# A hybrid S5, attention and mixture-of-experts layer: the scan dealt out in single instructions, biases later and on another queue, copies on another engine

## The chip, the cores and the metric

The kernel runs on one core of a Trainium2 chip. The metric is the device time of one execution in microseconds (us). The kernel before has a median of 1299.4 us over three runs (1301.35, 1297.85 and 1299.4).

The engines are named as the profile names them: PE is TensorE (PEld its weight loads), DVE is VectorE, ACT is ScalarE, POOL is GpSimd, SP is SyncE. In this kernel SP issues nearly all transfers and computes nothing; POOL issues a few.

## The reference, cut to what matters

There are 256 latent tokens and 256 context tokens of 1024 channels, one layer, batch 1, all in float32.

```python
h  = modulate(rmsnorm(x, norm1_g), sh1, sc1)        # sh, sc, g: from silu(c) @ w_mod + b_mod
hc = modulate(rmsnorm(ctx, norm1_g), sh1c, sc1c)
proj = h @ w_in            # columns: S5 input 512 | K 128 | V 128 | Q 512 | gates 2048
y = s5_mixer(proj[:, :512], ...)    # diagonal complex scan, 32 groups x 64 states, both directions
o = attention(q, k_all, v_all)      # 8 heads of 64, 2 KV heads, 512 keys, softmax
s = gelu(y); s = s * sigmoid(s @ w_glu + b_glu)
merged = sigmoid(gate_a) * (s @ w_ssm_out) + sigmoid(gate_b) * (o @ w_attn_out)
x = x + g1 * (merged @ w_out)
h2 = modulate(rmsnorm(x, norm2_g), sh2, sc2)
f = top-4-of-32 experts: gu = h2 @ w_gate_up[e] + b_gate_up[e]
                         act = (clip(up) + 1) * clip(gate) * sigmoid(1.702 gate)
                         act @ w_down[e] + b_down[e], weighted
out = rmsnorm(x + g2 * f, final_norm_g)
```

The experts' weights are 32 times 12 MB and are the bulk of the traffic.

## The kernel before

**Stages.** A first part (to about 135 us) loads x, ctx and the small parameters, builds the tables of the S5 part, and projects the S5 input, K, V and Q. A long middle part, the loop `for u in range(16)`, interleaves the gate projection with attention and with the S5 part. Then come a tail of attention chunks, eight *branches* (four output pieces of `w_ssm_out`, four of `w_attn_out`, each 24 matmuls), the output projection, the router, and the 32 experts.

**Memory.** There are 24 pages of 1 MB (128 x 2048 float32). A fixed list of transfers, the stream, holds every large weight tile in order of use: 8 gate tiles of `w_in`, `w_glu`, the tiles of `w_ssm_out`, `w_attn_out` and `w_out`, then the experts. When a page is given back (`release`, `used`), the next item of the stream is loaded into it by a DMA on SP. SP works through its DMAs in program order (`load`, L104), so a DMA that waits for a page holds up those behind it.

**Order.** From the middle part on, PE, DVE and ACT keep the order in which the program is written (`Pinned`, L49; `tmatmul`, L97; `ttrans`, L100). The rows of the profile therefore carry these helpers' lines, and what an instruction is must be told from its operands and its shape.

**Exactness.** A product is made of three fp32r products of halves: ACT copies a weight tile into a rounded `hi`, DVE subtracts it to get `lo`, and `mm3` issues hi*hi, hi*lo, lo*hi. A gate tile has two halves of 128 output columns, called units 0 to 15. A unit is 24 matmuls and needs two hi copies on ACT and two lo subtractions on DVE, each 128x512 (`gate_split`), a unit ahead of its use (`next_split`). `wsplit` does the same for the eight pieces n = 0 to 7 of the branches, with one copy and one subtraction of 128x1024. Its two buffers alternate, so the copy of piece n waits until PE has finished branch n - 2.

**The loop.** A unit u does, in this order: the normalization of the last attention chunk (`attn_norm`: reciprocal and multiply on DVE, then PE transposes), the split for unit u+1, `gate_mm` of its own unit, a modulation tile, and further pieces. From u = 3 on it does one attention chunk c = u - 3: score matmuls, row maximum on DVE (`smx`, the reduce), exp on ACT. The S5 scan stands in it as follows. At u = 2, `scan_up` issues 20 DVE instructions in a row (five levels of `cmul_add`, of 1024 columns falling to 64). From u = 3 to 9 the *pieces* follow, four DVE instructions at a time, two or three times a unit. At u = 10 the rest and `scan_out` follow: two copies of 64x992 on DVE and two on ACT, which lay out the states for the readout. At u = 11 `shift_logits` takes a small transposed copy, `shT`, to PE.

**Biases.** `bias_steps` is a generator. For n = 0, 1 (`b_gate_up`) and 2 (`b_down`) it issues three loads of 128 KB on POOL into one buffer, then makes, for each of two column halves, a bf16 copy on ACT, a subtraction on DVE, a copy, a subtraction and a copy. Each depends on the one before. The loop takes one step of it at each of three places per unit from u = 3 on, and what is left after it. The sums are needed only by the experts. POOL's queue also holds the 24 transfers of `Rd`, by which a kernel of the S5 part is spread over the partitions.

Of the kernel before, what the change touches and what calls it, by code (L numbers as in the profile page):

```python
# [12 lines left out]
F32R = mybir.dt.float32r  # L13
# [16 lines left out]
P_QT, P_M, P_A, P_SU, P_S, P_RO, P_RT, P_GL, P_BP = 2, 10, 3, 3, 10, 12, 14, 15, 3  # L30
# [3 lines left out]
def hybrid_block(ctx: ExitStack, tc: tile.TileContext, a: dict, out: bass.AP):  # L34
# [720 lines left out]
    S.activation(hH.bitcast(F32R), hT[1], AF.Copy)  # L755
    V.tensor_sub(hL.bitcast(F32R), hT[1], hH)
# [4 lines left out]
    mod_load(2)  # L761
    kv_proj(1, 1)
    mod_tile(False)
    w_tables(4)
    renew(13, "r")
    renew(10, "r")

    wgh, wgl_ = [pg(p_).rearrange("p (j k f) -> p j k f", j=2, k=8) for p_ in (13, 10)]

    def gate_split(i, j, parts=(0, 1)):  # L770
        for part in parts:
            for k in range(0, 8, GK):
                sl = slice(k, k + GK)
                src, hi, lo = loaded["gate", i][:, sl, 128 * j:128 * j + 128], wgh[:, j, sl], wgl_[:, j, sl]
                if part:
                    V.tensor_sub(lo.bitcast(F32R), src, hi)
                else:
                    S.activation(hi.bitcast(F32R), src, AF.Copy)

    gate_split(0, 0)  # L780
    gate_split(0, 1)
    used("gate", 0)
# [93 lines left out]
    def cmul_add(h_out, h_in, v_in, lv, n, t1, t2):  # L876
        lr_ = LS[:, lv, 0].unsqueeze(1).to_broadcast([128, n, 2, 32])
        li_ = LS[:, lv, 1].unsqueeze(1).to_broadcast([128, n, 2, 32])
        V.tensor_mul(t1, h_in, lr_)
        V.tensor_mul(t2, h_in[:, :, ::-1], li_)  # L880
        V.tensor_add(t1, t1, v_in)
        V.tensor_add(h_out, t1, t2)
# [15 lines left out]
    vb = vv[1].rearrange("p (b i) r g -> p i b r g", i=4)  # L900
    Sb, Hb, tb1, tb2 = [pg(8, 512 * i, 512).rearrange("p (s r g) -> p s r g", s=8, r=2) for i in range(4)]

    def scan_pieces():
        for i in range(1, 4):
            yield lambda i=i: cmul_add(Sb, Sb if i > 1 else vb[:, 0], vb[:, i], 0, 8, tb1, tb2)
        for b in range(8):
            if b:
# [3 lines left out]
        for i in range(3):  # L911
            yield lambda i=i: cmul_add(vb[:, i], vb[:, i - 1] if i else Hb, vb[:, i], 0, 8, tb1, tb2)
# [876 lines left out]
```

## Time and profile before

| | before |
|---|---|
| median of 3 runs | 1299.4 us |
| the profiled execution | 1298.59 us |
| its span, first to last instruction | 1296.9 us |
| mean granted clock of TensorE | 0.977 |
| busy PE / DVE / ACT | 90% / 32% / 14% |
| DMA moved | 462.55 MB, mean 357 GB/s |

All times of the trace count from the start of the span. The views used below are the page's chain of waits (the work that ended last, followed back from the end), the same chain in a stretch of time, a table of stretches (busy time of each engine, granted clock, DMA), the timeline of one engine (start, busy time, what it is, count, and in brackets the idle time before it and what ended that), the groups of instructions by line and shape, and the DMA issues. Instructions of one engine overlap a little, so that a row's duration can be some 0.1 us longer than the distance to the next row.

### The profile page before, as it was taken

Reading aid. Unit: us, or ns where it says so; the run is one execution under the profiler, and the core shown is the slowest. Engines: PE = TensorE matmul, PEld = TensorE weight load, DVE = VectorE, ACT = ScalarE, POOL = GpSimd, SP = SyncE. Lnnn points to the kernel's source line nnn. Section 1 sums busy time; section 2 is a strip of 40 time slices with the busy share of each in tenths; the row PEclk is TensorE's granted clock in tenths of the full one; section 3 lists DMA queues with packets and bytes.
Section 4 is the critical chain, followed back from the end, with each engine's and each line's share of the span. In section 5 each row is a group of like instructions: output and inputs, shape, how many; then the busy total and the mean of one; then the engine's idle time right before and its main releaser. Section 6 shows DMA issues by size and latency. Waiting matters only on the chain.

```text
span 1296.9 us, 16241 instructions
## 1 busy us (share of the span) xinstructions
PE 1172.1 (90%) x6791; PEld 540.0 (42%) x6792; DVE 414.5 (32%) x893; ACT 181.9 (14%) x350; POOL 50.0 (4%) x80
## 2 busy tenths in 40 slices
PE   3999685889989999999999998989898989899886
PEld 2775474769633333333333232323232323233224
DVE  4998886565322111211111211112111111111211
ACT  3142243552110000000000000000000000000001
POOL 1201032002000000000000000000000000000000
PEclk9999887989989999999999999999999999999998
DMA  9957267478799999999999999999999999999995
GB/s 279 311 192 251 99 144 145 151 284 338 273 376 418 417 417 418 417 417 417 417 416 417 417 417 417 418 417 417 417 418 417 418 416 417 416 417 416 416 386 194
DMA packets 119135, 462.55 MB, mean 357 GB/s; under 512 B 20669, under 2 KB 42345, under 8 KB 84242
## 3 DMA queue, kind: packets, MB, share of 16 engines
q1 hardware_dynamic: 117138, 457.13, 89.6%
q0 software_dynamic: 1872, 4.33, 1.6%
q8 instruction: 55, 0.90, 0.3%
q14 instruction: 22, 0.18, 0.0%
q10 hardware_dynamic: 48, 0.01, 0.0%
HBM read 459.89 MB, written 1.54 MB: 356 GB/s over the span
## 4 chain that ended last, share of the span: by engine, by line
DMA 45%; PE 43%; DVE 7%; ACT 2%; issue 2%; POOL 0%; SPq 0%; DVEq 0%; POOLq 0%; ACTq 0%
PE bk L97 41%; DMA pg<-in_w_gate_up_dram 28%; DMA pg<-in_w_down_dram 16%; DVE pg L49 5%; PE bk L100 3%; ACT pg L49 2%; DMA pg<-in_b_gate_up_dram 1%; DMA pg<-in_w_mod_dram 1%; DVE smx L49 1%; ACT L49 0%; DVE rsn_t L49 0%; DVE rs_t L49 0%; DVE gate L49 0%; DVE ssum L49 0%; DVE gs__2716 L49 0%
## 5 line engine op out<-in xcount | busy, mean ns | idle before, releaser
L97 PE MATMUL bk<-pg,pg 128*64 128x512 f32 (+7 forms) x5456 | 1004.7, 470 | 70.9 <-DMA pg<-in_w_down_dram 29.5
L97 PEld LDWEIGHTS bk<-pg,pg 128*64 128x64 f32 (+3 forms) x5456 | 452.1, 152 | 565.0 <-issue 360.9
L49 ACT ACTIVATE pg<-bk 128x512 f32<-128x512 f32 (+4 forms) x154 | 76.3, 522 | 746.2 <-PE bk L100 677.9
L49 DVE TENSOR_SCALAR pg<-bk 128x512 f32<-128x512 f32 x64 | 44.2, 691 | 295.3 <-PE bk L97 295.3
L49 DVE TENSOR_TENSOR pg<-pg,pg 128x1024 f32<-128x1024 f32 (+9 forms) x144 | 122.8, 881 | 36.5 <-ACT pg L49 33.3
L49 ACT ACTIVATE pg<-pg 128x512 f32<-128x512 f32 (+9 forms) x118 | 76.5, 670 | 263.3 <-DVE pg L49 231.5
L49 DVE TENSOR_TENSOR pg<-bk,shT 128x512 f32<-128x512 f32 x32 | 22.1, 691 | 268.1 <-PE bk L97 268.1
L49 DVE TENSOR_TENSOR pg<-bk,pg 128x512 f32<-128x512 f32 (+4 forms) x52 | 32.1, 619 | 227.7 <-PE bk L97 224.5
L100 PE MATMUL bk<-ident,pg 128*128 128x128 f32 x448 | 72.8, 291 | 21.4 <-DVE pg L49 14.0
L100 PEld LDWEIGHTS bk<-ident,pg 128*128 128x128 f32 x448 | 50.8, 145 | 82.7 <-issue 43.0
L97 PE MATMUL bk<-pg 64*128 64x512 f32 (+1 forms) x368 | 70.3, 484 | 0.0
L97 PEld LDWEIGHTS bk<-pg 64*128 64x128 f32 (+1 forms) x368 | 19.9, 159 | 50.0 <-issue 50.0
L49 DVE TENSOR_TENSOR pg<-pg 128x512 f32<-128x512 f32 (+3 forms) x89 | 37.3, 434 | 3.8 <-ACT pg L49 3.0
L1643 POOL DMA_DIRECT2D pg<-g2d x2 | 1.3, 642 | 883.8 <-PE bk L97 883.8
L97 PE MATMUL bk<-pg,selB 128*64 128x512 bf16 (+1 forms) x196 | 34.4, 388 | 0.0
L49 DVE SCALAR_TENSOR_TENSOR pg<-pg 128x512 f32<-128x512 f32 (+3 forms) x67 | 30.3, 458 | 6.6 <-DMA pg<-in_x_dram 4.8
L97 PE MATMUL bk<-pg,scond 128*32 128x256 f32 (+1 forms) x256 | 27.4, 525 | 2.5 <-DMA pg<-in_w_mod_dram 2.5
L49 DVE TENSOR_SCALAR pg<-iot,posp,gate 128x128 f32<-128x128 f32 x64 | 18.9, 339 | 0.0
L49 ACT ACTIVATE pg<-bk,smx 128x512 f32<-128x512 f32 x16 | 11.0, 688 | 35.9 <-DVE smx L49 35.8
L49 DVE TENSOR_SCALAR pg<-iot,posp,rs 128x64 f32<-128x64 f32 x64 | 15.7, 307 | 0.1
L97 PEld LDWEIGHTS <-selB 128*64 128x64 bf16 x196 | 9.0, 109 | 16.1 <-issue 15.9
L49 DVE COPY pg<-bk 128x512 f32<-128x512 f32 (+1 forms) x24 | 14.5, 610 | 3.4 <-PE bk L100 2.9
(151 smaller groups left out, 192.0 us busy)
## 6 DMA issues: line engine op xcount, KB each, us to landing
pg<-in_w_gate_up_dram SPq DMA_DIRECT2D x256, 1024.0 KB, 19.9
pg<-in_w_down_dram SPq DMA_DIRECT2D x127, 1024.0 KB, 20.1
pg<-in_w_mod_dram SPq DMA_DIRECT2D x16, 1024.0 KB, 5.9
pg<-in_w_in_dram SPq DMA_DIRECT2D x13, 1024.0 KB, 10.1
pg<-in_w_mod_dram SPq DMA_DIRECT2D x16, 512.0 KB, 9.4
pg<-in_w_out_dram SPq DMA_DIRECT2D x4, 1024.0 KB, 8.2
pg<-Rd POOLq DMA_DIRECT2D x16, 128.0 KB, 11.0
pg<-in_w_ssm_out_dram SPq DMA_DIRECT2D x2, 1024.0 KB, 5.1
```

The costliest lines, as they stand in the source:

```text
L49: i = f(*ar, **kw)
L97: pinned(T.matmul(*ar, **kw))
L100: pinned(T.transpose(*ar))
L1643: G.dma_start(late["g2"][:, 512 * j:512 * j + 512], g2d[j:j + 1].to_broadcast([128, 512]))
```

## The change

- **Scan.** `scan_up` and the pieces become one generator that yields after every DVE instruction. `scan_some(22)` takes instructions until their columns (in units of 64, plus 2 for each) come to 22: once at u = 2, twice a unit from u = 3 on, the rest at u = 10.
- **Whole gate tiles.** `N_WHOLE = 2`: units 0 to 3 multiply the loaded tile with `hT[1]` in plain float32, eight matmuls a unit, without a split. The split ahead of `q_proj(0)` goes; the split of h (`hH`, `hL`, 128x2048) moves from ahead of `kv_proj(0, 1)` to u = 1 (ACT) and u = 2 (DVE). Pages 13 and 10 carry modulation tiles in the meantime, and modulation tiles stand at other units. The biases of the modulation (`mod_bias`) move to u = 4.
- **Split order.** The hi copies of unit u+1 now stand ahead of `attn_norm` on ACT.
- **Copies.** The multiply of `attn_norm` moves from DVE to ACT; the two large copies of `scan_out` move from DVE to ACT, and two small ones from ACT to DVE.
- **Biases.** The loads go by SP. The steps begin at u = 9 (two a unit), go on with four after each branch's `wsplit`, and the rest stands after the branches. The zeroing on POOL is done once.

Cut to its core, with the loop's rows for modulation and the old page renewals left out:

```diff
-P_QT, P_M, P_A, P_SU, P_S, P_RO, P_RT, P_GL, P_BP = 2, 10, 3, 3, 10, 12, 14, 15, 3
+P_QT, P_M, P_A, P_S, P_RO, P_RT, P_GL, P_BP, P_B, P_SC, N_WHOLE = 2, 10, 3, 10, 12, 14, 15, 3, 9, 22, 2
...
-    S.activation(hH.bitcast(F32R), hT[1], AF.Copy)
-    V.tensor_sub(hL.bitcast(F32R), hT[1], hH)
     kv_proj(0, 1)
...
-    gate_split(0, 0)
-    gate_split(0, 1)
-    used("gate", 0)
     q_proj(0)
...
             for p in (0, 2, 3):
-                load_g(raw[32 * p:32 * p + 32], src)
-            for _ in range(4):
+                load(raw[32 * p:32 * p + 32], src)
+            for _ in range(3):
                 yield
...
     def cmul_add(h_out, h_in, v_in, lv, n, t1, t2):
-        V.tensor_mul(t1, h_in, lr_)
+        yield V.tensor_mul(t1, h_in, lr_), n
...
+    def scan_some(cols):
+        while cols > 0:
+            step = next(scan_left, None)
+            if step is None:
+                return
+            cols -= step[1] + 2
...
     def scan_out():
         for r in range(2):
-            V.tensor_copy(Hn[0:64, :, r, 1:32].rearrange("p g c -> p c g"), vv[1][0:64, 0:31, r])
+            S.activation(Hn[0:64, :, r, 1:32].rearrange("p g c -> p c g"), vv[1][0:64, 0:31, r], AF.Copy)
...
-            S.activation(Hn[64:128, :, r, 31:32].rearrange("p g c -> p c g"), h0[64:128, :, r], AF.Copy)
+            V.tensor_copy(Hn[64:128, :, r, 31:32].rearrange("p g c -> p c g"), h0[64:128, :, r])
...
         for k in range(8):
-            mm3(gbk[0][:, 256 * j:256 * j + 256], wgh[:, j, k], wgl_[:, j, k], hH[:, k], hL[:, k], k == 0, k == 7)
+            o = gbk[0][:, 256 * j:256 * j + 256]
+            if i < N_WHOLE:
+                mm(o, loaded["gate", i][:, k, 128 * j:128 * j + 128], hT[1][:, k], k == 0, k == 7)
+            else:
+                mm3(o, wg[0][:, j, k], wg[1][:, j, k], hH[:, k], hL[:, k], k == 0, k == 7)
...
-        V.tensor_scalar(pb, pb, ssum[:, c_i:c_i + 1], None, op0=ALU.mult)
+        S.activation(pb, pb, AF.Copy, scale=ssum[:, c_i:c_i + 1])
...
     for u in range(16):
+        next_split(u + 1, 0)
         attn_norm(n_attn - 1)
-        if u:
-            next_split(u + 1, 0)
-        if P_SU <= u < P_S:
-            n_scan = scan_some(1)
-        if u:
-            next_split(u + 1, 1)
+        next_split(u + 1, 1)
+        if u > 2:
+            scan_some(P_SC)
         gate_mm(u // 2, u % 2)
-        if u > 2:
-            next(bias_left, None)
...
         if u == P_QT:
             for i in range(2):
                 q_T(i)
                 k_T(i)
-            scan_up()
-        if P_SU <= u < P_S:
-            n_scan = scan_some(1)
+            V.tensor_sub(hL.bitcast(F32R), hT[1], hH)
+        if u > 1:
+            scan_some(P_SC)
...
-        if u > 2:
+        if u >= P_B:
             next(bias_left, None)
...
-    for _ in bias_left:
-        pass
...
         wsplit()
+        for _ in range(4):
+            next(bias_left, None)
...
+    for _ in bias_left:
+        pass
     release(0, 1, 10, 13)
```

Three places show how this moves instructions. The first is DVE between the transposes of q and k (u = 2) and the splits that follow. Before, these are the end of the scan's first part and its first piece (pg_68 and pg_62 are its pages, LS its multipliers), and behind them the lo subtractions of unit 3 (pg_1004):

```order
L49 TENSOR_TENSOR LS<-pg_62 128x64 [waits DVE_49]
L49 TENSOR_TENSOR pg_68<-pg_69,LS 128x512 x2
L49 TENSOR_TENSOR pg_68<-pg_68,pg_69 128x512 [waits DVE_49]
L49 TENSOR_TENSOR pg_68<-pg_68 128x512 [waits DVE_49]
L49 TENSOR_TENSOR pg_1004<-pg_83,pg_1003 128x512 [waits DMAHW5_49,DMAHW2_49,Activation_49]
L49 TENSOR_TENSOR pg_1004<-pg_83,pg_1003 128x512 [waits Activation_49]
```

After, with pg_309 as `hL` and pg_1243 as the lo buffer:

```order
L49 TENSOR_TENSOR pg_309<-pg_63,pg_308 128x2048
L49 TENSOR_TENSOR pg_62<-pg_68,LS 128x1024 x2
L49 TENSOR_TENSOR pg_1243<-pg_82,pg_1242 128x512 [waits DMAHW7_49,DMAHW3_49,Activation_49]
L49 TENSOR_TENSOR pg_1243<-pg_82,pg_1242 128x512 [waits Activation_49]
L49 TENSOR_TENSOR pg_62<-pg_62,pg_68 128x1024 [waits DVE_49]
L49 TENSOR_TENSOR pg_68<-pg_62 128x16x64 [waits DVE_49]
L49 TENSOR_TENSOR pg_79<-bk_1151,Dm 128x4x16 [waits DMAHW1_49,Activation_49,Pool_49]
```

Two instructions of the scan now stand ahead of the lo subtractions (of unit 4) where there were 24, and `hL` stands ahead of both.

The second is ACT at u = 10 and 11, around `scan_out` (64x31x32 are its large copies, pg_67<-pg_63 are bias copies, the 128x512 rows ending in pg_83 or pg_82 the hi copies of the next split). Before:

```order
L49 ACTIVATE pg_65,ssum<-bk_1927,smx 128x512 [waits DVE_49]
L49 ACTIVATE pg_67<-pg_63 128x512
L49 ACTIVATE pg_68<-pg_69 64x31x32
L49 ACTIVATE pg_68<-LS 64x32
L49 ACTIVATE pg_68<-pg_69 64x31x32
L49 ACTIVATE pg_68<-LS 64x32
L49 ACTIVATE pg_1003<-pg_83 128x512 [waits DMAHW6_49,PE_49]
L49 ACTIVATE pg_1003<-pg_83 128x512 [waits PE_49]
```

After:

```order
L49 ACTIVATE pg_65,ssum<-bk_1825,smx 128x512 [waits DVE_49]
L49 ACTIVATE pg_67<-pg_63 128x512 [waits DMAHW1_49,DMAHW7_49,DMAHW0_49,Pool_49]
L49 ACTIVATE pg_68<-pg_69 64x31x32 [waits DVE_49]
L49 ACTIVATE pg_68<-pg_69 64x31x32 x3
L49 ACTIVATE pg_1242<-pg_82 128x512 [waits DMAHW6_49,PE_49]
L49 ACTIVATE pg_1242<-pg_82 128x512 [waits PE_49]
L49 ACTIVATE pg_65<-pg_65,ssum 128x512 [waits DVE_49]
```

All four large copies are now on ACT, ahead of the hi copies.

The third is branch 3. On SP before, behind the split of piece n = 5 (pg_71 is the page that it frees):

```order
L104 DMA pg_71<-in_w_gate_up_dram 128x2048 [waits DMAHW6_49,DVE_49]
L104 DMA pg_68<-in_w_gate_up_dram 128x2048 [waits DMAHW7_49]
L104 DMA pg_2568<-in_w_gate_up_dram 128x2048 [waits DMAHW0_49,PE_49]
L104 DMA pg_72<-in_w_gate_up_dram 128x2048 [waits DMAHW1_49,DVE_49]
L104 DMA pg_66<-in_w_gate_up_dram 128x2048 [waits DMAHW2_49,DVE_49]
```

After:

```order
L104 DMA pg_71<-in_w_gate_up_dram 128x2048 [waits DMAHW4_49,DVE_49]
L104 DMA pg_63<-in_b_down_dram 32x1024 [waits DMAHW5_49]
L104 DMA pg_63<-in_b_down_dram 32x1024 [waits DMAHW6_49]
L104 DMA pg_63<-in_b_down_dram 32x1024 [waits DMAHW7_49]
L104 DMA pg_68<-in_w_gate_up_dram 128x2048 [waits DMAHW0_49]
```

The three loads of `b_down` now stand behind the tile that waits for DVE. And ACT after, from the hi copy of n = 5 (pg_71) to the second of pg_72, which is n = 7; the rows with pg_67 did not stand here before:

```order
L49 ACTIVATE pg_1242<-pg_71 128x1024 [waits PE_49]
L49 ACTIVATE pg_67<-pg_63 128x512 [waits DMAHW7_49,DMAHW6_49,DMAHW5_49]
L49 ACTIVATE pg_1242<-pg_72 128x1024 [waits PE_49]
L49 ACTIVATE pg_67<-pg_63 64x512 [waits DVE_49,Activation_49]
L49 ACTIVATE pg_67<-pg_63 32x512 [waits DVE_49]
L49 ACTIVATE pg_1242<-pg_72 128x1024 [waits PE_49]
```

Between the hi copies of n = 5 and n = 6 there is now a copy that waits for those three loads, and between n = 6 and n = 7 there are two that wait for DVE.

## Rows read from the trace of the kernel before

**Rows 1.** The page: the chain that ended last, shares by engine.

```profile
DMA 45%; PE 43%; DVE 7%; ACT 2%; issue 2%; POOL 0%; SPq 0%; DVEq 0%; POOLq 0%; ACTq 0%
```

**Rows 2.** Stretches: us, their length, busy PE, PEld, DVE, ACT, POOL, clock, DMA.

```profile
165.00:205.00 40.00, 33.70 (x383) 26.95 (x382) 34.93 (x84) 18.08 (x37) 14.45 (x26) 0.88 0.78 164
320.00:340.00 20.00, 20.00 (x136) 15.99 (x135) 9.70 (x29) 5.59 (x20) 0.00 (x0) 1.00 0.70 253
370.00:380.00 10.00, 10.00 (x54) 4.17 (x50) 1.21 (x3) 0.00 (x0) 0.00 (x0) 0.98 0.75 266
400.00:700.00 300.00, 297.71 (x1444) 106.94 (x1445) 54.37 (x109) 17.71 (x33) 0.00 (x0) 1.00 1.02 417
...
222.00:224.00 2.00, 1.47 (x7) 1.47 (x8) 1.99 (x4) 0.77 (x2) 0.64 (x2) 0.50 0.77 240
```

**Rows 3.** The chain in order of time, 590 to 720 us: start, length, what.

```profile
597.04 14.52 PE bk L97 x74
...
651.10 14.52 PE bk L97 x74
...
678.28 18.21 DMA pg<-in_w_gate_up_dram
```

**Rows 4.** Timeline of PE, 150 to 312 us.

```profile
163.48 6.05 PE L97 MATMUL bk<-pg,pg 128*128 128x256 f32 x56 [9.86 <-DVE pg L49]
...
222.53 1.12 PE L100 MATMUL bk<-ident,pg 128*128 128x128 f32 x4 [10.87 <-DVE pg L49]
223.30 4.72 PE L97 MATMUL bk<-pg,pg 128*128 128x256 f32 x24
...
280.10 3.12 PE L97 MATMUL bk<-pg,pg 128*128 128x256 f32 x24
```

**Rows 5.** Timeline of DVE, 146 to 240 us.

```profile
148.73 2.35 DVE L49 TENSOR_TENSOR pg<-pg,LS 128x1024 f32<-128x1024 f32 x2
...
162.00 1.29 DVE L49 TENSOR_TENSOR pg<-pg,pg 128x512 fp32r<-128x512 f32 x2
...
165.87 0.68 DVE L49 TENSOR_REDUCE smx<-bk 128x1 f32<-128x512 f32 x1
...
215.43 0.69 DVE L49 TENSOR_TENSOR pg<-pg,pg 64x512 f32<-64x512 f32 x1 [9.41 <-ACT pg L49]
...
223.00 0.68 DVE L49 TENSOR_REDUCE smx<-bk 128x1 f32<-128x512 f32 x1
...
224.30 1.06 DVE L49 COPY pg<-pg 64x992 f32<-64x992 f32 x1
...
231.59 0.17 DVE L49 COPY shT<-bk 128x8 f32<-128x8 f32 x1
```

**Rows 6.** Timeline of ACT, 200 to 240 us.

```profile
214.76 0.63 ACT L49 ACTIVATE pg<-pg 128x512 bf16<-128x512 f32 x1 [12.59 <-DMA pg<-in_b_gate_up_dram]
...
226.88 1.95 ACT L49 ACTIVATE pg<-pg 64x992 f32<-64x992 f32 x1
```

**Rows 7.** Groups by line and shape, 96 to 320 us: busy, mean ns | idle before.

```profile
L49 ACT ACTIVATE pg<-pg 128x512 fp32r<-128x512 f32 x34 | 19.4, 622 | 1.6 <-PE bk L97 1.5
...
L49 DVE TENSOR_SCALAR pg<-pg,ssum 128x512 f32<-128x512 f32 x16 | 8.6, 540 | 0.6
```

**Rows 8.** Timelines of ACT, SP and DVE in the branches.

```profile
295.21 1.06 ACT L49 ACTIVATE pg<-pg 128x1024 fp32r<-128x1024 f32 x1 [2.53 <-PE bk L97]
298.09 1.06 ACT L49 ACTIVATE pg<-pg 128x1024 fp32r<-128x1024 f32 x1 [1.82 <-PE bk L97]
...
297.56 35.23 SPq L104 DMA_DIRECT2D pg<-in_w_gate_up_dram  x13
...
308.20 0.69 DVE L49 SCALAR_TENSOR_TENSOR pg<-pg,pg 128x512 f32<-128x512 f32 x1
```

**Rows 9.** DMA issues: KB each, median us to landing; 270 to 320 us, then all.

```profile
pg<-in_w_gate_up_dram SPq DMA_DIRECT2D x13, 1024.0 KB, 7.3
...
pg<-in_b_down_dram POOLq DMA_DIRECT2D x3, 128.0 KB, 3.2
```

More of the change, by code (lines that the diff above doesn't have):

```diff
@@ L760, in hybrid_block, with gate_split @@
     mod_tile()
-    mod_load(2)
     kv_proj(1, 1)
-    mod_tile(False)
+    mod_tile()
+    mod_load(13)
     w_tables(4)
[L765 to L778, printed above, removed]
-    gate_split(0, 0)
-    gate_split(0, 1)
-    used("gate", 0)
+    wg = {}
+    def gate_split(i, j, part):
+        if not wg:
+            renew(13, "r")
+            renew(10, "r")
+            wg[0], wg[1] = [pg(p_).rearrange("p (j k f) -> p j k f", j=2, k=8) for p_ in (13, 10)]
+        for k in range(0, 8, GK):
+            sl = slice(k, k + GK)
+            src, hi, lo = loaded["gate", i][:, sl, 128 * j:128 * j + 128], wg[0][:, j, sl], wg[1][:, j, sl]
+            if part:
+                V.tensor_sub(lo.bitcast(F32R), src, hi)
+            else:
+                S.activation(hi.bitcast(F32R), src, AF.Copy)
     q_proj(0)
@@ L886, in hybrid_block, with scan @@
     h0 = LS[:, 4, 0:1]
-    def scan_up():
+    vb = vv[1].rearrange("p (b i) r g -> p i b r g", i=4)
+    Sb, Hb, tb1, tb2 = [pg(8, 512 * i, 512).rearrange("p (s r g) -> p s r g", s=8, r=2) for i in range(4)]
+    def scan():
         cur = vv[0]
@@ L964, in gate_mm @@
         for k in range(8):
-            mm3(gbk[0][:, 256 * j:256 * j + 256], wgh[:, j, k], wgl_[:, j, k], hH[:, k], hL[:, k], k == 0, k == 7)
+            o = gbk[0][:, 256 * j:256 * j + 256]
+            if i < N_WHOLE:
+                mm(o, loaded["gate", i][:, k, 128 * j:128 * j + 128], hT[1][:, k], k == 0, k == 7)
+            else:
+                mm3(o, wg[0][:, j, k], wg[1][:, j, k], hH[:, k], hL[:, k], k == 0, k == 7)
+        if i < N_WHOLE and j:
+            used("gate", i)
         if j:
@@ L1013, in hybrid_block, with mod_bias @@
     bmr = pg(3, 1024, 1024).rearrange("p (i f) -> p i f", i=2)
-    G.memset(bmr, 0.0)
-    for q in range(4):
-        G.dma_start(bmr[32 * q:32 * q + 1],
-                    w("b_mod")[2048:6144].rearrange("(i q f) -> q i f", i=2, q=4)[q:q + 1])
+    def mod_bias():
+        G.memset(bmr, 0.0)
+        for q in range(4):
+            G.dma_start(bmr[32 * q:32 * q + 1],
+                        w("b_mod")[2048:6144].rearrange("(i q f) -> q i f", i=2, q=4)[q:q + 1])
     M = [None, bmr[:, 0], bmr[:, 1]]
@@ L1188, in next_split @@
     def next_split(u, part):
-        if u < 16:
-            gate_split(u // 2, u % 2, (part,))
+        if 2 * N_WHOLE <= u < 16:
+            gate_split(u // 2, u % 2, part)
             if part and u % 2:
                 used("gate", u // 2)
-    n_attn, n_scan = 0, 0
-    def scan_some(n):
-        end = min(n_scan + n, len(pieces))
-        scan_steps(n_scan, end)
-        return end
+    n_attn = 0
     for u in range(16):
+        next_split(u + 1, 0)
         attn_norm(n_attn - 1)
-        if u:
-            next_split(u + 1, 0)
-        if P_SU <= u < P_S:
-            n_scan = scan_some(1)
-        if u:
-            next_split(u + 1, 1)
+        next_split(u + 1, 1)
+        if u > 2:
+            scan_some(P_SC)
         gate_mm(u // 2, u % 2)
-        if u > 2:
-            next(bias_left, None)
-        if u == 0 or (u % 2 and mods["done"] < 16):
-            mod_tile(u > 0)
+        if u < 3 or (u % 2 == 0 and mods["done"] < 16):
+            mod_tile(u > 1)
         if 2 <= u < 6:
@@ L1222, in hybrid_block @@
             q_split()
+            S.activation(hH.bitcast(F32R), hT[1], AF.Copy)
         if u == P_QT:
```

37 lines of the change are left out of this document (16 added, 21 removed).

## The prediction

> **What bounds the kernel now.** I read the page's chain of waits first. It gives DMA 45% and PE 43% of the end [rows 1], so the next question is where one hands over to the other. The stretches answer it. From 400 us on DMA is busy all the time at 417 GB/s, but from 320 to 340 us it moves 253 GB/s, and from 370 to 380 us 266 GB/s [rows 2]: there it waits for pages that TensorE has yet to free. The chain at 590 to 720 us agrees. A pair of experts takes TensorE 651.10 - 597.04 = 54.06 us, and only at 678.28 does a transfer take the chain over [rows 3]. So up to about 380 us the transfers follow TensorE, and after that they never pause. A microsecond that the part ahead of the experts gains or loses is therefore gained or lost at the end, one for one. The whole question is how long that part is.
>
> In it TensorE stands still twice. It waits 9.86 us for VectorE until 163.48, and 10.87 us until 222.53 [rows 4]. The first wait is the first level of the scan, 20 instructions in one row that VectorE begins at 148.73; the weight split that TensorE needs follows only at 162.00 [rows 5]. The second is a bias: ScalarE waits 12.59 us until 214.76 for the DMA of `b_gate_up` [rows 6], and VectorE, whose next subtraction needs that copy, waits 9.41 us [rows 5]. At 222 us the granted clock stands at 0.50 [rows 2], the lower of its two levels (1.2 GHz of 2.4): 24 matmuls of a gate, like those that take 3.12 us at 280.10, take 4.72 at 223.30 [rows 4].
>
> **The change, part by part.** I follow the row maximum of the softmax (the reduce, one per unit) as a milestone. Before, c0 stands at 165.87, c7 at 223.00, and the copy of `shT` at 231.59 [rows 5].
>
> *Scan dealt out, gate tiles whole.* The block of the scan no longer stands ahead of a split, and gate_mm(4) is the first that needs a split at all, so TensorE goes on at once: c0 comes some 8 us sooner. From there VectorE is the longer engine, so I sum its work from 148.73 to c7, where before it took 223.00 - 148.73 = 74.3 us. Off come the wait for the bias (9.4), seven norm multiplies (0.54 each by the mean [rows 7], less where instructions overlap: together 3.3) and the two subtractions of unit 3's split at 162.00 (1.3 [rows 5]). q_T comes about 1 us earlier, since the first split ahead of q_proj is gone. On come 2.3 us, the 128x2048 subtraction of `hL` (an estimate: 4 x 0.65, the half row at 162.00, less overlap). That is -12.7. Two smaller things follow from the orders: the hi copies now stand ahead of the norm on ScalarE (VectorE waited for them in most units, together some 1.6 us), and the last modulation tile is fetched ahead of the traffic of POOL's queue: 0 to -1.5. I take **-14** for c7 (bounds: -11, if ScalarE, which now holds the norms too, makes VectorE wait a further 0.5 us in six units; -15.5). The scan itself isn't made smaller: what leaves the block comes back in units 3 to 9. The whole tiles cost TensorE 0.6 us a unit in four units; three of them lie beside VectorE's work.
>
> *Biases off POOL's queue.* The loads leave the queue behind the shared kernel's transfers; they are issued about two units ahead of the first copy. The 9.4 us are in the sum above.
>
> *Copies to ScalarE.* At u=10 the two large copies of scan_out go from VectorE to ScalarE, where there are now four in a row, and the hi copies of the next split and with them `shT` stand behind the fourth. Such a copy of 64x992 took ScalarE 1.95 us [rows 6]. From c7 to `shT` before: 231.59 - 223.00 = 8.6. After: reduce and transposed copy 1.3, rest of the scan 1.9 (three instructions like those of [rows 5]), four copies 7.8, two hi copies 1.2 (0.622 each [rows 7]), half a lo 0.65, and handovers: 13.0. So **+4.4**. TensorE then stands for some 11 us, as long as at 222.53, and pays for its clock what it paid there: (4.72 - 3.12) and the transposes, **+2.1** (0 to 2.5).
>
> The Trainium skill, "ScalarE: Activation LUTs", section "What ACT_TABLE_LOAD costs", says that an ACTIVATE with immediate operands takes 186 ns + 0.833 ns a column; by it such a copy would be 1.01 us, an estimate, and the four 4.1 instead of 7.8. The trace says 1.95. The page's "Rules for kernel authors" would leave multiplies to VectorE, against this move; by it nothing more than the rows above is priced.
>
> *The norm on ScalarE in the tail.* From c13 on there are no splits beside it. The multiply stands in the chain maximum, exp, norm, transpose, now 0.62 (a ScalarE instruction of 512 columns) instead of 0.54 [rows 7], with a handover to another engine, and behind whatever ScalarE has: +1.0. In branches 1 and 2 it stands behind a bias copy: +0.9.
>
> *Biases in the branches.* Here I expect the loss. Four steps of the bias follow each branch's weight split. The orders show that branch 3 issues the three loads of `b_down` on SP behind a 1 MB expert tile, which itself waits for the subtraction of n=5, and that ScalarE's copy of that bias, later in the same branch's steps, stands ahead of the hi copy of n=6. Take E as the end of branch 3's matmuls, 295.21 before, when the hi copy of n=5 starts [rows 8]. The subtraction then ends, and the tile was issued at 297.56, E + 2.35 [rows 8]. Around it, 1 MB tiles land 7.3 us after issue in the median (over a shared link), 128 KB of `b_down` on POOL 3.2 [rows 9]. DMA was idle at that moment, so I take 2.5 us for the megabyte at 417 GB/s, 2 for the way and 1 for the three small ones: landed at E + 7.8. Copy 0.6, hi of n=6 1.06, lo 1.25 and handovers: E + 11.0. TensorE has done branches 4 and 5 at E + 5.8, since a branch takes 2.9 (298.09 - 295.21 [rows 8]), and waits 5.2 for branch 6. Then come two subtractions and two copies of the bias, of 0.63 and 0.69 each [rows 5, 6], in turn on both engines, ahead of the split of n=7: branch 7 starts at E + 15.8 instead of E + 8.6, 7.2 late. VectorE's own steps for the gates pile up behind: the last was at 308.20, E + 13.0 [rows 8]; now E + 22.2. **+9.2** (bounds: +3.2, if the bias lands before ScalarE comes to it and only the turns remain; +12, if it takes as long as a tile in the median). Branch 1's turns ahead of n=5 add 1.1.
>
> The sum: -14 + 4.4 + 2.1 + 1.0 + 0.9 + 1.1 + 9.2 = **+4.7**. On the profiled execution, 1298.6 us (a span of 1296.9 and what lies around it), that is 1303.3; the median of the runs is 0.8 above that execution: 1304.1, I say **1304**.
>
> **The rivals.**
> *The bias lands in time.* SP runs ahead where it can; if the three loads cross the tile or the wait is shorter than I have it, branch 3 costs 3.2 and not 9.2: 1304 - 6 = 1298. Against it: SP takes its queue in order, and the tile ahead waits for VectorE. Chance 0.2.
> *The first half gains more, and the end is faster.* The place is units 3 to 9. Before, TensorE ran at half clock after each wait, and VectorE waited for exp in most units; if TensorE goes through without a pause, the exp and hi copies are done before VectorE comes to them, c7 gains 18 and not 14, and the pause at `shT` is shorter than the gate that it falls back by. With a short stall of 5 in the branches, it is 1304 - 4 - 2 - 4 = 1294. It decides as soon as c7 is at 205 or earlier and branch 7's matmuls start less than 4 us late. Against it: the scan's own 11 us are still to be done by an engine that is busy 34.9 of 40 us [rows 2]. Chance 0.17.
> *Half clock in the units.* If VectorE leaves TensorE waiting 2 to 3 us in every unit, the 0.50 clock of [rows 2] stays on in units 6 to 10, and each gate costs up to 1.6 more where TensorE is the later one: about two units, +3, 1307. Chance 0.13.
> *The copies are cheap.* ScalarE's 1.95 us stood beside VectorE's copies into the same page, and VectorE's first, which began ahead of them, took 1.06 [rows 5]. If they slowed each other, four on one engine take about 1.06 each: 7.8 - 4.2 = 3.6 less, 1300. Against it: ScalarE's second copy [rows 6] ran mostly after VectorE's last large one, and took its 1.95 all the same. Chance 0.05. (The page named above would have it so.)
> *The change doesn't remove the wait but moves it*, from POOL's queue to SP's: that is my forecast, chance 0.45.
>
> **How the numbers follow.** About 0.3% (3.9 us) is what a measurement of this kernel tells from no change. The forecast's own cases spread over 1300 to 1310, about two thirds above 1303.3. With the rivals: slower 0.33 + 0.13 + a little of the others = 0.48; same 0.12 + 0.15 + 0.05 = 0.32; faster 0.05 + 0.15 = 0.2. The unknown costs together run from -15.5 + 4.4 + 1 + 3.2 = -6.9 (1292.5) to -11 + 8 + 4 + 12 = +13 (1312); leaving out the corners, the range is 1294 to 1310.
>
> **What would show it.** After, the scan's levels should lie between the splits, and TensorE should have no wait over 3 us between 150 and c7. c7's reduce should be at 207 to 211; four 64x992 copies on ScalarE of 1.9 us each, `shT` 13 us behind c7, and the 24 matmuls after it at 4 to 5 us. In the branches, ScalarE should wait some 4 us for `in_b_down_dram`, and TensorE 5 us for VectorE ahead of branch 6; the first matmuls of the out projection should end 3 to 7 us later than before. From 400 us on nothing should differ but the offset. The forecast is wrong if ScalarE's wait for `b_down` is under 1 us, if c7 is outside 205 to 213, or if the offset at the first expert doesn't come back at the end.

## The result and the profile after

The changed kernel takes 1305.27 us in the median of five runs (1304.6 to 1309.45), the kernel before 1297.85 over five. The ratio is 1.0058, with a 95% interval of 1.0037 to 1.0080: 7.5 us slower. The forecast was 1304, slower with a chance of 0.48, in a range of 1294 to 1310.

The profiled execution took 1309.45 us, with a span of 1307.7. It is the longest of the five, so its times are compared by distances, not by where they stand. The kernel was profiled once more among the experiments, in an execution of 1307.72 us; where two numbers stand with a slash, the second is from there.

The page's chain is now, by engine:

```profile
PE 56%; DMA 32%; DVE 6%; ACT 3%; issue 2%; SPq 1%; POOL 0%; ACTq 0%; DVEq 0%; POOLq 0%
```

The stretch from 400 to 700 us reads as in [rows 2], with DMA busy throughout at 417 GB/s:

```profile
400.00:700.00 300.00, 299.24 (x1456) 107.92 (x1452) 56.25 (x111) 19.63 (x35) 0.00 (x0) 1.00 1.02 417
```

Here are the milestones of [rows 5, 8] in the timeline of VectorE (start, busy time, what): c0, c7, `shT`, the last gate step, and the first addition that takes a result of the output projection.

```profile
159.26 0.68 DVE L49 TENSOR_REDUCE smx<-bk 128x1 f32<-128x512 f32 x1
...
212.37 0.68 DVE L49 TENSOR_REDUCE smx<-bk 128x1 f32<-128x512 f32 x1
...
225.21 0.17 DVE L49 COPY shT<-bk 128x8 f32<-128x8 f32 x1
...
319.05 0.69 DVE L49 SCALAR_TENSOR_TENSOR pg<-pg,pg 128x512 f32<-128x512 f32 x1
...
324.49 0.69 DVE L49 TENSOR_TENSOR pg<-bk,pg 128x512 f32<-128x512 f32 x1 [4.72 <-PE bk L97]
```

The last of these stood at 313.83 before:

```profile
313.83 0.69 DVE L49 TENSOR_TENSOR pg<-bk,pg 128x512 f32<-128x512 f32 x1 [4.92 <-PE bk L97]
```

It is 10.66 us late, and the execution is 1309.45 - 1298.59 = 10.86 us longer: what the first 325 us lose comes out at the end, one for one, as the chain said.

TensorE's waits of over 3 us, in its timeline, are these (before there were the two of [rows 4] and 3.36 us ahead of `shT`'s product):

```profile
157.59 4.63 PE L97 MATMUL bk<-pg,pg 128*128 128x256 f32 x24 [3.85 <-DVE pg L49]
...
193.58 1.94 PE L97 MATMUL bk<-pg,scond 128*32 128x512 f32 x8 [6.57 <-DMA pg<-in_w_mod_dram]
...
211.91 1.12 PE L100 MATMUL bk<-ident,pg 128*128 128x128 f32 x4 [4.43 <-DVE pg L49]
212.68 4.72 PE L97 MATMUL bk<-pg,pg 128*128 128x256 f32 x24
...
225.43 1.01 PE L97 MATMUL bk<-rw_sb,shT 128*1 128x32 f32 x16 [7.59 <-DVE shT L49]
...
305.70 0.80 PE L97 MATMUL bk<-pg,pg 128*128 128x256 f32 x2 [5.53 <-ACT pg L49]
```

The waits of 9.86 and 10.87 us are gone, and so is ScalarE's 12.59 us. Others stand in their place: for a modulation tile, for VectorE ahead of c7, for `shT`, and for ScalarE in the branches. For such a tile TensorE had waited before too, but less:

```profile
202.57 1.51 PE L97 MATMUL bk<-pg,scond 128*32 128x512 f32 x8 [2.01 <-DMA pg<-in_w_mod_dram]
```

ScalarE's timeline shows what it did in the branches: the copy of n = 5, then 8.15 us of standing for `b_down`.

```profile
294.86 1.06 ACT L49 ACTIVATE pg<-pg 128x1024 fp32r<-128x1024 f32 x1
304.07 1.58 ACT L49 ACTIVATE pg<-pg 128x512 bf16<-128x512 f32 x2 [8.15 <-DMA pg<-in_b_down_dram]
```

And SP's timeline shows the loads that it stood for, issued directly behind the 1 MB tile:

```profile
297.21 0.33 SPq L104 DMA_DIRECT2D pg<-in_w_gate_up_dram  x1
297.59 1.52 SPq L104 DMA_DIRECT2D pg<-in_b_down_dram  x3
```

The milestones give five distances, and the experiments are read by them. All are us, from starts in VectorE's timeline; "out" is the first addition behind the output projection. The rows below the first two are the kernels of the experiments.

| | c0 to c7 | c7 to shT | shT to c13 | c13 to last gate step | last step to out |
|---|---|---|---|---|---|
| before | 57.13 | 8.59 | 42.57 | 34.04 | 5.63 |
| changed, twice | 53.11 / 52.73 | 12.84 / 12.83 | 44.27 / 44.51 | 49.57 / 50.01 | 5.44 / 5.43 |
| `b_down` copied late | 52.60 | 12.72 | 44.08 | 42.06 | 8.49 |
| two copies on VectorE | 53.69 | 8.84 | 44.69 | 50.33 | 5.44 |
| transfers on SP, unit 9 | 50.86 | 12.80 | 43.64 | 51.19 | 5.44 |
| scan's first part in a row | 46.93 | 13.70 | 44.06 | 49.59 | 5.44 |
| norm on VectorE | 53.16 | 12.84 | 43.58 | 47.59 | 5.44 |
| biases on POOL, early | 65.47 | 13.65 | 46.57 | 35.72 | 5.71 |
| three edits | 51.60 | 8.85 | 43.73 | 42.28 | 7.12 |
| four edits | 52.01 | 8.85 | 42.95 | 40.18 | 8.77 |
| four edits, more steps in units | 51.41 | 8.86 | 46.13 | 36.36 | 5.56 |
| before, norm on ScalarE | 55.57 | 9.21 | 46.80 | 36.46 | 5.71 |
| before, four copies on ScalarE | 57.71 | 12.33 | 44.71 | 33.96 | 5.71 |

c0 itself stands at 165.87 before and at 159.26 / 157.19 in the changed kernel. It varies from one execution to the next: over the profiles of kernels whose program is the same up to there it lies between 154.65 and 160.36. So a difference of 2 or 3 us in where c0 stands tells nothing. The profiled execution need not be the typical one either: that of `scanout_dve` is the slowest of its ten, that of `bdown_late` among the faster ones of its ten.

### The profile page after: what moved, and what is told of

It is laid out like the page before. It is cut to its first block, busy times and chain, and to the rows that moved or that the text cites. A ratio compares the mean times of both kernels' runs of the same rounds, so it can differ in the third digit from the quotient of the medians.

```text
span 1307.7 us, 16152 instructions
## 1 busy us (share of the span) xinstructions
PE 1180.8 (90%) x6759; PEld 543.2 (42%) x6760; DVE 401.4 (31%) x869; ACT 191.3 (15%) x358; POOL 43.2 (3%) x69
## 4 chain that ended last, share of the span: by engine, by line
PE 56%; DMA 32%; DVE 6%; ACT 3%; issue 2%; SPq 1%; POOL 0%; ACTq 0%; DVEq 0%; POOLq 0%
PE bk L97 53%; DMA pg<-in_w_gate_up_dram 28%; DVE pg L49 5%; PE bk L100 3%; ACT pg L49 3%; DMA pg<-in_w_mod_dram 2%; DMA pg<-in_w_down_dram 2%; SPq L104 1%; DMA pg<-in_b_down_dram 0%; DMA pg<-in_w_out_dram 0%; DVE smx L49 0%; ACT L49 0%; DVE rsn_t L49 0%; DVE rs_t L49 0%; DVE gate L49 0%
## 5 line engine op out<-in xcount | busy, mean ns | idle before, releaser
L97 PE MATMUL bk<-pg,pg 128*64 128x512 f32 (+6 forms) x5424 | 1012.4, 473 | 68.8 <-DMA pg<-in_w_down_dram 27.9
L49 DVE TENSOR_TENSOR pg<-pg,pg 128x1024 f32<-128x1024 f32 (+8 forms) x136 | 118.9, 901 | 46.3 <-ACT pg L49 44.5
L49 DVE TENSOR_TENSOR pg<-pg,LS 128x64 f32<-128x64 f32 (+4 forms) x36 | 15.6, 472 | 0.4
## 6 DMA issues: line engine op xcount, KB each, us to landing
pg<-Rd POOLq DMA_DIRECT2D x16, 128.0 KB, 12.2
```

What stands on the lines that cost most here:

```text
L49: i = f(*ar, **kw)
L97: pinned(T.matmul(*ar, **kw))
```

## The experiments

Each is named by its label and by its edit. "Before" in a ratio is the kernel before, timed on the same chip in the same rounds.

**The changed kernel again** (`after_again`, no edit).

> The changed kernel once more, for a second profile: the first profiled execution, 1309.45 us, was the longest of five (median 1305.27). The account by paths says that the gates' last row on VectorE, 319.05 us there, again stands 1:1 with the time, so an execution of 1305 should have it near 315, with the 4 us gone from one of the two transfers that TensorE waits for (the last modulation tile, 15.5 us on its way, or b_down, for which ScalarE waited 8.15 us). The rival, that the spread comes from the experts, has it at 319 again with another time.

Measured: 1306.46 us, ratio 1.0058 (1.0039 to 1.0078); the profiled execution took 1307.72. The last gate step is at 317.27 and "out" at 322.70, 1.79 us ahead of the first profile, and that execution was 1.73 us shorter: the 1:1 account holds. But neither transfer took the difference: TensorE's wait for the tile was 6.23 us and ScalarE's for `b_down` 8.17. It was there at c0 already (157.19, 2.07 earlier). The spread between executions lies ahead of 150 us, and that part of the expectation failed.

**`b_down` copied late** (`bdown_late`): the loads stay, the first copy comes eight steps later.

```diff
-            for _ in range(3):
+            for _ in range(3 if n < 2 else 11):
                 yield
```

> The changed kernel, with ScalarE's first copy of b_down eight steps later, which is behind the weight splits of pieces 6 and 7; the loads stay where they are. If the stall of the branches is ScalarE standing in its queue for b_down (8.15 us) and the turns behind it, TensorE's wait of 5.5 us ahead of branch 6 goes, and the time falls by 8 to 11 us, to about 1296. The rival, that the branches were late through VectorE's queue of gate steps and bias subtractions whatever the copy waits for, gives 1303 to 1305 with the wait gone and the last gate step as late as before.

Measured: 1299.57 us, ratio 1.0005 (0.9991 to 1.0020): 6.9 us faster than the changed kernel, a little under the 8 expected. TensorE's wait ahead of branch 6 is gone, and from c13 to the last gate step it is 7.5 us less, of which 3.05 come back behind it. ScalarE still waits for the same bias, but with the splits of n = 6 and 7 already behind it:

```profile
299.47 0.63 ACT L49 ACTIVATE pg<-pg 128x512 bf16<-128x512 f32 x1 [2.82 <-DMA pg<-in_b_down_dram]
...
307.04 0.69 DVE L49 SCALAR_TENSOR_TENSOR pg<-pg,pg 128x512 f32<-128x512 f32 x1
```

The last gate step at 307.04 still has bias subtractions and their turns ahead of it on VectorE. The output projection comes 3 us later behind it (8.49 instead of 5.44): TensorE had waited twice ahead of it (1.08 and 2.42 us, the changed kernel's 1.33 and 0.19), and it ran at the lower level of its clock from 308 us on, the changed kernel at the full one:

```profile
308.00:312.00 4.00, 4.00 (x10) 3.19 (x11) 0.00 (x0) 0.45 (x2) 0.00 (x0) 0.50 1.02 426
```

```profile
318.00:322.00 4.00, 3.34 (x14) 2.65 (x15) 1.73 (x4) 0.00 (x0) 0.00 (x0) 1.00 0.90 334
```

So the place of the copy in ScalarE's queue was worth 6.9 us by the medians; by the distances from c0 to "out" it was 5.3 to 5.6.

**Two copies on VectorE** (`scanout_dve`).

```diff
-            S.activation(Hn[0:64, :, r, 1:32].rearrange("p g c -> p c g"), vv[1][0:64, 0:31, r], AF.Copy)
+            V.tensor_copy(Hn[0:64, :, r, 1:32].rearrange("p g c -> p c g"), vv[1][0:64, 0:31, r])
```

> The changed kernel with two of the four large copies of the scan's output back on VectorE, two left on ScalarE. If ScalarE's row of four is what shT waits for, then from c7's row maximum to shT it takes 8.6 to 9.2 us instead of 12.8, the 7.6 us wait of TensorE falls to about 3.5, the half clock behind it goes, and the time falls by 4 to 6.5 us, to about 1300. The rival, that the 4 us come back as VectorE's own time (its two copies took 2.9 us before), gives 1304 to 1305.

Measured: 1301.17 us, ratio 1.0015 (1.0001 to 1.0030): 5.3 us faster. c7 to `shT` is 8.84 us, and TensorE's wait is 3.41:

```profile
218.53 1.01 PE L97 MATMUL bk<-rw_sb,shT 128*1 128x32 f32 x16 [3.41 <-DVE shT L49]
```

The row of four copies is what `shT` waited for. The clock was still at its lower level behind this wait, against the expectation; before, it was at the full one:

```profile
231.81 0.63 PE L97 MATMUL bk<-rw_sb,shT 128*1 128x32 f32 x16 [3.36 <-DVE shT L49]
```

From c0 to "out" this profile is only 2.2 to 2.5 us shorter than the changed kernel's two, less than the 5.3 of the medians. It comes from the slowest of the ten executions; whether the clock was at the full level in the faster ones isn't shown.

**The 16 transfers on SP at unit 9** (`kernel_in_sp`).

```diff
-                load_g(Kt[hf][16 * i:16 * i + 16],
+                load(Kt[hf][16 * i:16 * i + 16],
...
-            kernel_in()
...
+        if u == 9:
+            kernel_in()
```

> The changed kernel with the 16 transfers that spread the S5 part's kernel over the partitions issued by SP at unit 9, behind the last modulation tile, instead of by POOL from unit 5 on. If the crowd of these transfers is what made the last modulation tile take 15.5 us, it takes about 6 (the median of such tiles), TensorE's wait of 6.6 us at 193.6 goes, c7 comes 2 to 4 us earlier (VectorE takes over as the limit), and the time falls by 2 to 4 us, to about 1302. The rival, that VectorE's work sets c7 alone, has the wait gone and c7 at 212 as before: 1305.

Measured: 1303.78 us, ratio 1.0035 (1.0018 to 1.0052): 2.7 us faster. TensorE no longer waits for a modulation tile, and c0 to c7 is 50.86 us, 1.9 to 2.3 less. That is less than the wait of 6.57, since VectorE is then the later one: TensorE's wait ahead of c7 grows from 4.43 to 7.91 us.

```profile
210.76 1.11 PE L100 MATMUL bk<-ident,pg 128*128 128x128 f32 x4 [7.91 <-DVE pg L49]
```

In the changed kernel's chain the tile stands as a step of its own, 15.49 us from issue to landing, where the median of such tiles is 5.9; the transfers beside it are of 128 KB each and take 12.2 us in the median:

```profile
178.04 15.49 DMA pg<-in_w_mod_dram
```

```profile
pg<-Rd POOLq DMA_DIRECT2D x16, 128.0 KB, 12.2
```

With the edit, by then behind the tile, they take 7.8 us:

```profile
pg<-Rd SPq DMA_DIRECT2D x16, 128.0 KB, 7.8
```

**The scan's first part in a row** (`scan_block`).

```diff
-        if u > 1:
+        if u == 2:
+            for _ in range(20):
+                next(scan_left)
+        if u > 2:
             scan_some(P_SC)
```

> The changed kernel with the first 20 instructions of the scan in one row again (at unit 2, behind hL), the rest dealt out as it is. If VectorE's whole work sets c7, the row delays c0 by 6 to 8 us and gives it back by c7, because less of the scan is left for the units: c7 within 2 us of the changed kernel's distance from unit 2, and the time 1306 to 1308. The rival, that dealing the scan out is itself the gain (TensorE works on while VectorE scans), leaves c7 5 to 8 us late: 1311 to 1314.

Measured: 1309.67 us, ratio 1.0083 (1.0055 to 1.0112): 3.2 us slower than the changed kernel, between the two theories. TensorE waits for the row as it did in [rows 4]:

```profile
163.51 5.45 PE L97 MATMUL bk<-pg,pg 128*128 128x256 f32 x24 [12.08 <-DVE pg L49]
```

Counted from the subtraction of `hL`, c0 comes 8.3 us later, but c0 to c7 is 6 us shorter. From that subtraction (146.95 here, 149.25 / 147.18 in the changed kernel) to c7 it is 65.3 us against 63.1 / 62.7, so of the 8 us that TensorE gains at c0, about 2.4 are left at c7. With the 0.9 us by which `shT` comes later behind c7, that is the 3.2 us. The first theory was closer: VectorE's work decides, and what leaves the row comes back in the units.

**The norm on VectorE** (`norm_dve`).

```diff
-        S.activation(pb, pb, AF.Copy, scale=ssum[:, c_i:c_i + 1])
+        V.tensor_scalar(pb, pb, ssum[:, c_i:c_i + 1], None, op0=ALU.mult)
```

> The changed kernel with the attention's norm multiply back on VectorE. By the account it costs VectorE 0.4 to 0.5 us in each of the seven units (c0 to c7: 53 us becomes 55 to 56) and gives back in the tail and the branches: from shT to the hi copy of piece 2 52 to 53 us instead of 54 to 55, from there to the copy of piece 5 14 to 15 instead of 15.6. Together 1304 to 1307. The rival, that the whole loss of branches 1 to 3 is the norm on ScalarE, gives 12 to 12.5 us there, and 1302 to 1303.

Measured: 1302.19 us, ratio 1.0032 (1.0015 to 1.0049): 3.4 us faster by the ratios, 4.3 by the medians. The tail and the branches are 2.7 us shorter: from `shT` to the hi copy of n = 2 it is 52.80 us, from there to n = 5 14.12, as expected. The units didn't become longer: c0 to c7 is 53.16 us, as with the norm on ScalarE. VectorE's timeline shows why. In the changed kernel, between a reciprocal and the subtraction of the next split:

```profile
175.26 0.16 DVE L49 RECIPROCAL ssum<-ssum 128x1 f32<-128x1 f32 x1 [0.85 <-ACT pg L49]
176.26 1.29 DVE L49 TENSOR_TENSOR pg<-pg,pg 128x512 fp32r<-128x512 f32 x2 [0.84 <-ACT pg L49]
```

and with the multiply back:

```profile
170.99 0.17 DVE L49 RECIPROCAL ssum<-ssum 128x1 f32<-128x1 f32 x1 [0.84 <-ACT pg L49]
171.19 0.49 DVE L49 TENSOR_SCALAR pg<-pg,ssum 128x512 f32<-128x512 f32 x1
172.00 1.29 DVE L49 TENSOR_TENSOR pg<-pg,pg 128x512 fp32r<-128x512 f32 x2 [0.32 <-ACT pg L49]
```

The distance from reciprocal to subtraction is 1.00 and 1.01 us. VectorE has to wait there for the hi copy anyway, and the multiply stood in that wait for nothing. In the other units it is the same: from c0 to c7 the seven such distances are 0.51 to 1.28 us without the multiply and 0.60 to 1.28 with it, together 0.33 us more. With TensorE's wait for the modulation tile gone, the seven multiplies cost little too: c0 to c7 is 52.01 us with them on VectorE and 51.60 without (the four edits and the three edits below).

**The biases as before** (`bias_pool`): loads on POOL, a step at three places of each unit from 3 on, the rest ahead of the branches.

```diff
-                load(raw[32 * p:32 * p + 32], src)
-            for _ in range(3):
+                load_g(raw[32 * p:32 * p + 32], src)
+            for _ in range(4):
...
-        if u >= P_B:
+        if u > 2:
             next(bias_left, None)
...
```

> The changed kernel with the biases as before: loads on POOL, three steps a unit from unit 3 on, all done ahead of the branches. By the account the two distances in the branches return to 12 to 13 us each (from 15.6 and 24.2: -14), and ScalarE's wait for b_gate_up behind POOL's queue returns at c5 to c6 (+8 to 11, c0 to c7 61 to 64 us): 1300 to 1303. The rival, that the move of the biases is a gain as a whole (the wait at c6 costs more than the branches), gives 1307 or more.

Measured: 1306.13 us, ratio 1.0063 (1.0044 to 1.0083): the same as the changed kernel, and outside the 1300 to 1303. From the hi copy of n = 2 to that of n = 5 it is 12.74 us and from there to the last gate step 12.91, as expected; from c13 to the last gate step 35.72, 13.9 less. But c0 to c7 is 65.47, 12.4 more, and the step of the expectation that failed is who waits there: not ScalarE for the bias but TensorE for the modulation tile, which took 23.9 us from issue to landing, where it took 15.5 in the changed kernel.

```profile
201.08 1.93 PE L97 MATMUL bk<-pg,scond 128*32 128x512 f32 x8 [12.08 <-DMA pg<-in_w_mod_dram]
```

So the move of the biases is worth nothing as a whole: what it gives ahead of c7 it takes in the branches. That holds with the 16 transfers on POOL's queue beside the tile; how much of the 12.4 us is left without them was not tried.

**Three edits together** (`combo1`): the late copy of `b_down`, two copies on VectorE, the 16 transfers on SP.

> Three of the edits together: the copy of b_down eight steps later, two of the scan's output copies back on VectorE, and the 16 transfers on SP at unit 9. If the three losses lie one behind the other on the path, they add up: 1306.5 - 6.9 - 5.3 - 2.7 = 1291.5, within 2 us. The rival, that they hide one another (a wait that goes uncovers the next), gives 1295 or more.

Measured: 1294.81 us, ratio 0.9967 (0.9952 to 0.9982): 11.7 us faster than the changed kernel, 1.3 us above the range for a plain sum. By the distances of the table, the part from c0 to "out" is 153.6 us instead of 165.2 / 165.5: also 11.7 to 11.9. By the same distances the single edits gave 5.3 to 5.6, 2.2 to 2.5 and 1.3 to 1.6 us, together 8.8 to 9.7. So the profiles don't show that the edits hide one another; the single gains by the medians, each with an interval of some 2 us to either side, sum to 14.9. Part of the difference can be the clock: behind `shT` it was at the lower level in all three single profiles, and at the full one here.

```profile
215.47 0.63 PE L97 MATMUL bk<-rw_sb,shT 128*1 128x32 f32 x16 [3.70 <-DVE shT L49]
```

**Four edits** (`combo2`): these and the norm on VectorE.

> The three edits of before together with the norm multiply on VectorE. If the norm's 4.3 us lie on the path behind the others, 1294.8 - 4.3 = 1290.5, within 2 us. The rival, that VectorE is now the limit in units 3 to 9 and takes the multiply on its path, gives 1294 or more.

Measured: 1290.13 us, ratio 0.9947 (0.9930 to 0.9963), as expected from a sum.

**Four edits and more steps in the units** (`combo3`): in place of the eight steps of `bdown_late`:

```diff
-            for _ in range(3):
+            for _ in range((3, 7, 9)[n]):
                 yield
...
+        if u >= 11:
+            for _ in range(4):
+                next(bias_left, None)
```

> As the kernel with the four edits, but with four more bias steps at the end of each unit from 11 on, and longer waits between loads and copies of the second and third bias, so that no step is left for the last four branches. If the steps between the splits are what keeps the two distances in the branches above those of the kernel before (15.6 against 12.1, 16.7 against 13.0), the second goes to 13 and the time falls by another 3 to 4 us, to 1287. The rival, that units 11 to 15 grow by as much, gives 1290 to 1292.

Measured: 1287.97 us, ratio 0.9928 (0.9906 to 0.9950), 1 us above the first theory and 2 below the rival. The second distance in the branches is 13.5 us. The distance from c13 to the last gate step falls by 3.8 us to 36.36 and the one behind it by 3.2 to 5.56, as before the change (the clock there is at 1.00 again, where it was at 0.50 from 304 to 308 us with the four edits); but `shT` to c13 grows by 3.2. About half of the steps' cost went into the units. The gain over the four edits is inside the two intervals; over the kernel before it is 0.7%, over the changed kernel 1.3%.

**The kernel before with one part of the change.** `before_norm_act` has the norm on ScalarE:

> The kernel before, with the attention's norm multiply on ScalarE and nothing else changed. In the changed kernel, putting it back on VectorE gave 4.3 us. If the loss lies in the chain maximum, exp, norm, transpose of the tail, it needs no bias steps beside it: c0 to c7 57 us as before, from shT to the hi copy of piece 2 53 to 54 us instead of 51.5, and 1301 to 1303 against 1298.3. The rival, that it cost only together with the biases in the branches, gives 1298 to 1299.

Measured: 1302.41 us, ratio 1.0033 (1.0015 to 1.0051), 4.3 us slower. `shT` to c13 is 4.2 us longer and c13 to the last gate step 2.4, with no bias step in the branches; from `shT` to the hi copy of n = 2 it is 57.6 us, more than the 53 to 54 expected. Not all of the 4.2 us is the norm: the clock was at its lower level behind `shT` here (1.01 us for the 16 products, after a wait of 3.38), and with it `shT` to c13 is 2.1 us longer in the next run too, whose norm is on VectorE. On the other side, the wait for the bias ahead of c7 was shorter (6.77 us instead of 12.59), without which the time would show more. So the move costs by itself, but how much isn't settled by this run.

`before_scanout_act` has the four large copies on ScalarE:

> The kernel before, with all four large copies of the scan's output on ScalarE (and the two small ones on VectorE), as in the change, and nothing else. From c7's row maximum to shT 8.6 becomes 12.8 us, TensorE's wait ahead of shT 3.4 becomes 7.6, the clock is at 0.50 behind it: 4 to 6.5 us in all, 1302 to 1305. The rival, that ScalarE has room for them where the biases' loads are on POOL, gives under 1300.

Measured: 1302.69 us, ratio 1.0041 (1.0026 to 1.0056), 5.3 us slower. TensorE's wait ahead of `shT`'s product is as in the changed kernel, and so is the clock behind it; c7 to `shT` is 3.7 us longer and `shT` to c13 2.1:

```profile
236.48 1.01 PE L97 MATMUL bk<-rw_sb,shT 128*1 128x32 f32 x16 [7.42 <-DVE shT L49]
```

## Why the prediction was right, and where it was not

The direction and the size held: slower, by +4.7 on the profiled execution in the sum and by 7.5 (4.8 to 10.4) measured. Not every term did.

- *What bounds it.* Right. The part ahead of the experts moves the end one for one, in both profiles and in the edits: the time less the place of "out" is 983.3 to 986.1 us in all fourteen profiles.
- *c7, -14.* c7 stood 10.6 us earlier (212.37) in the first profile and 13.1 (209.92) in the second. The first lies just outside the bounds of -11 to -15.5; both lie inside 205 to 213. The size was about right, its make-up was not, and that is in part luck. The seven norms, put at -3.3, gave nothing in the units (`norm_dve`): I had counted VectorE's busy time, and the multiply lay in a wait. The modulation tile, put at 0 to -1.5, was a loss: TensorE waits 6.57 us for it, where it waited 2.01 before. It was issued at 178.04, in the midst of POOL's transfers, which begin at 176.94, and not ahead of them. The tile was as long on its way before (issued at 187.11, used at 202.57); now TensorE comes to it sooner. Without the transfers beside it 1.9 to 2.3 us come back at c7 (`kernel_in_sp`). c0 came 6.6 / 8.7 us sooner, about the 8 of the forecast (the row of 20 instructions ahead of it is five levels of the scan, not the first alone), and c0 to c7 fell by 4.0 / 4.4 where the forecast leaves 6. Two terms that miss by more than 5 us together make the distance come out only some 2 short, so others in the sum were too small; no run shows which. The sign that TensorE has no wait over 3 us between 150 and c7 failed with this: it has three.
- *Copies to ScalarE, +4.4 and +2.1.* Right. c7 to `shT` took 12.84 us where I had 13.0, and the move costs 5.3 us both ways (`scanout_dve`, `before_scanout_act`). TensorE stood for 7.59 us ahead of `shT`'s product and not for 11, but the clock fell all the same, and in `before_scanout_act` `shT` to c13 is 2.1 us longer, which is that term. A copy took 1.91 us in the mean of four (the row stands below this list). That also ends the rival of the cheap copies: no large copy of VectorE stood beside these. The 1.01 us that comes from the Trainium skill, "ScalarE: Activation LUTs", section "What ACT_TABLE_LOAD costs", does not hold for this shape; the measurement decides.
- *The norm in the tail, +1.0 and +0.9.* The mechanism was right, the size too small: 3.4 by the ratios in the changed kernel, 4.3 us in the kernel before, part of which can be the clock. I priced it at one place of the chain; by the distances it costs 0.7 to 0.9 us from `shT` to c13 and 2.0 to 2.4 from c13 to the last gate step (`norm_dve` against the changed kernel's two profiles).
- *Biases in the branches, +9.2 and +1.1.* Right in its steps, 3.6 us short in size: c13 to the last gate step is 13.9 us longer than with the biases out of the branches (`bias_pool`), where the two terms made 10.3. Some 2 us of this lie behind E. With E at 294.86, the bias landed at E + 9.2 (I had 7.8), branch 6, of which two matmuls ran at 305.70, went on at 306.96, E + 12.1 (11.0), and the last gate step came at E + 24.2 (22.2). The landing was too small: its 2 us for the way stand in no row, and the three loads took 5.4 us each from issue to landing, where the row for POOL says 3.2. ScalarE's wait of 8.15 us was twice the "some 4" of the signs, which also don't follow from E + 7.8: ScalarE is done with n = 5 at E + 1.1. The rest lies ahead of E, where the distance from n = 2 to n = 5 is 15.58 us against 12.74 in `bias_pool`: 2.8 us for the turns that I put at 1.1. `bdown_late` gives back 6.9 us of it all.
- *The rivals.* None came true. The bias did not land in time; the first half gained no more than the sum; and the clock fell behind single waits (at 157.6, 193.6, 211.9 and 225.4 us), not in every unit. That TensorE ran at half clock after each wait before, as one rival has it, isn't so: behind the 3.36 us ahead of `shT`'s product it ran at the full level. That the change only moves a wait was the forecast, and `bias_pool` shows it at its plainest: with the biases as before, the changed kernel takes the same time.
- *The sum.* Measured by the distances of the two profiles, c7 came 3.4 / 0.9 us later than the -14, and from `shT` to "out" it took 17.0 / 17.7 us longer where the terms behind `shT` made 14.3. Both errors point the same way. The one of c7 is inside the spread of c0; the one behind `shT` is as large as the 2.8 us between 4.7 and 7.5.

```profile
L49 ACT ACTIVATE pg<-pg 64x992 f32<-64x992 f32 x4 | 7.6, 1909 | 1.3 <-DVE pg L49 1.3
```

By the single edits, with the ratios against the changed kernel: the norm +3.4, the copies +5.6, the biases 0, dealing the scan out -3.2. The copies and the norm, which were meant to free VectorE, sum to 9.0, about the whole loss of 7.5 us; no run takes back these two alone. What the whole gate tiles, the earlier hi copies and the new places of the modulation tiles give was not tried; if the single effects add up, about +1.7 is left for them, which is inside the intervals.

## What to carry to other kernels

An engine that is busy most of a stage still has waits in it, and an instruction that lies in such a wait costs nothing there: before moving work off the busiest engine, look at what stands ahead of the moved instruction's successor, not at its duration. On the engine that receives it, look at what is queued behind. A step that waits for a transfer belongs behind the work that the critical engine needs next; moving one copy eight steps down a queue was worth 7 us, while moving the loads to another queue and the steps to a later stage was worth nothing as a whole.

## What the runs showed that I had not expected

- The same wait ahead of `shT`'s product was followed by either level of the clock. The 16 products took 0.63 us (full clock) after waits of 3.36 (before), 3.70 (three edits) and 3.82 us (four edits), and 1.01 us after 3.41 (`scanout_dve`), 3.38 (`before_norm_act`) and 2.88 us (four edits, more steps in the units). The length of this wait alone does not decide it; what does is open.
- A 1 MB tile that took 5.9 us in the median took 15.5 us, and 23.9 in `bias_pool`, while 16 transfers of 128 KB were on their way from another engine's queue. Issued by SP, in the same queue and behind it, they took 7.8 us instead of 12.2.
- The spread between executions of the same program was already there at 150 us: up to 5.7 us at c0, and at most 0.44 us in the distances of the changed kernel's two profiles behind it (12.84 / 12.83 us, and 15.58 for both from the copy of n = 2 to that of n = 5).
